# A decoder block's down product as seven block products by Strassen's algorithm

## The chip, the core and the metric

The kernel runs on one core of a Trainium2 chip. A core has TensorE for matrix products (PE in the profile, PEld for its weight loads), VectorE (DVE), ScalarE (ACT) and GpSimd (POOL) for work on elements, and SyncE (SP), which here issues nearly all transfers between the core's memory and DRAM, in the order of its own queue. Each engine works through its own instructions in a fixed order and waits for the others by semaphores. The metric is the time of one execution in microseconds (us).

## The reference

One decoder block over 1024 tokens of width 1024 in float32: eight heads of sparse attention, eight stick-breaking heads, an output projection, and a gated MLP with a convolution of width 3 along the tokens. The part that is changed is the last product:

```
gate, val = up[..., :D_FF], up[..., D_FF:]
h = h + (jax.nn.silu(gate) * val) @ w_down[layer]     # (1024 x 2816) @ (2816 x 1024)
```

and then a final RMSNorm.

## The kernel before, in words

Products run in a reduced float32 form (fp32r). To keep the accuracy, each operand is split into a high half (a copy in fp32r, on ScalarE, L193) and a low half (the operand less the high half, L194), and a product is three matmuls: high by high, high by low, low by high.

The stages that matter here, in order of time:

**The stick-breaking heads** (`sb_attend`, 65 to 345 us). Four pairs of heads go through 48 chunks, numbered here from 1. For each chunk `sb_front` makes logits on TensorE, two sigmoids on ScalarE, a scan on VectorE (L436) and two multiplications on GpSimd (L439: `A <- A,tt`); two chunks later `sb_turn` transposes the products on TensorE (L455), and `sb_back` multiplies them with the values. Beside this, in the gaps of TensorE, the next pair's projections run (L219 to L221): their weights come by SP (L204, `wr <- w_in_d`), and GpSimd makes the low halves (`wl`, L194). So GpSimd has 96 multiplications `A` and the halves `wl` in one fixed order.

**The up stage** (`up`, to 1246 us) makes `act = silu(gate) * val`, 22 blocks of 128 of the 2816 columns, and stores them to `act_d` in DRAM. Its product already runs as seven block products.

**The down stage** (`down`, from 1246.6 us). Two passes over the tokens (c, 512 tokens each); in a pass eight accumulators in PSUM (four blocks of 128 tokens `tb`, two halves `hf` of 512 output columns) take 22 blocks `i` of the contraction, each with three matmuls:

```
nc.tensor.matmul(pd, ah[:, s], dh[:, cs], start=i == 0, stop=False)
nc.tensor.matmul(pd, ah[:, s], dl[:, cs], start=False, stop=False)
nc.tensor.matmul(pd, al[:, s], dh[:, cs], start=False, stop=i == NF - 1)
```

That is 2 x 22 x 8 x 3 = 1056 matmuls of 128 x 512. `load_w` loads 128 rows of `w_down` (`wr`) and splits them (`dh` on ScalarE, `dl` on GpSimd); `load_act` loads 512 tokens of one act block (`ar`) and splits them (`ah` on ScalarE, `al` on VectorE). The first four blocks of a pass and the last four run accumulator by accumulator, so that the ends can be finished one by one: add to `h` (L1622), squares, a power on GpSimd, scale, store (L1572).

A scheduler sets each engine's order when the kernel is built, and moves instructions ahead of others where it reckons that they are ready; a tile with one buffer is written again only when its last reader is done.

Of the kernel before, what the change touches and what calls it, by code (L numbers as in the profile page):

```python
# [10 lines left out]
F32 = mybir.dt.float32  # L11
F32R = mybir.dt.float32r
# [68 lines left out]
class Kern:  # L81
# [479 lines left out]
                    nc.vector.memset(self.score[rows, i, cur + 1:16], NEG)  # L561


    def compress_in(self, kv, wp, vp):

        nc, a = self.nc, self.a
        w = self.load_cols(wp, a["w_in"], (C_KC, C_VC)[kv], bufs=3, rbufs=2, parts=2)
        for c in range(2):
            pm = self.ps("mm")
            yield from self.mm3_steps(pm, [w[k] + self.u(k, c) for k in range(KT)])  # L570
            src = self.tl(vp, [P, 512], "vt")
            nc.scalar.activation(src, pm, AF.Copy)
            nc.sync.dma_start(self.kct_d[kv][:, c * 512:c * 512 + 512], src)
            yield
# [491 lines left out]
    def run(self):  # L1066
# [15 lines left out]
        with self.pool("sbv", "right") as vp:  # L1082
            st_b, st_a = ExitStack(), ExitStack()
            stk = [None, st_b.enter_context(self.pool("stkb", "right"))]
            stk[0] = st_a.enter_context(self.pool("stka", "right"))
            ops = []
            with self.pool("xin") as xin:
                proj = self.sb_project(0, wp, stk[0], vp, ops, xin)
                self.load_norm(xin, vp, mxs, proj, stk[1])
                for _ in proj:  # L1090
                    pass
            with self.pool("sbw") as work:
                fill, due = iter(()), 0.0
# [19 lines left out]
                for _ in fill:  # L1113
                    pass
            st_a.close()
            st_b.close()
# [148 lines left out]
    def mlp(self, mxs):  # L1265
# [125 lines left out]
        for _ in fill:  # L1391
            pass
        st_r.close()
        self.weights, self.acts = {}, {}
        self.up(p1)
        self.down(st_up)

# [58 lines left out]
    def up(self, p1):  # L1456
# [3 lines left out]
        for i in range(NF):  # L1460
# [34 lines left out]
            if last:  # L1495
                for _ in range(AHEAD):
                    self.prepare()
                self.load_w(0)
                self.load_w(1)
            bb = self.ps(tags[1])  # L1500
            self.product(bb, i, "P6", True)
            u2 = self.scratch()
# [3 lines left out]
            u3 = self.scratch()  # L1506
            nc.vector.tensor_add(u3, bc, u2)
            if last:
                for j in range(GROUP):
                    if j > 1:  # L1510
                        self.load_w(j)
                    self.load_act(j, 0)
            bd = self.ps(tags[3])
            self.product(bd, i, "P5", True)

# [14 lines left out]
            gate(1)  # L1530


    def load_w(self, i):

        homes = ((self.qn, 0), (self.qn, 4), (self.mts, 4), (self.mts, 0))
        if i < 2 * len(homes):
            if i in self.weights:
                return
            t, lo = homes[i // 2]
            v = t[:, lo:lo + 4].rearrange("p a b t -> p (a b t)")[:, 2048 * (i % 2):2048 * (i % 2) + 2048]  # L1540
            dh, dl = v[:, 0:T], v[:, T:2048]
        else:
            dh, dl = (self.tl(self.dp, [P, T], t, 5, F32R) for t in ("dh", "dl"))
        raw = self.tl(self.rawp, [P, KT, P], "wr", 4).rearrange("p k c -> p (k c)")
        self.nc.sync.dma_start(raw, self.a["w_down"][i * P:(i + 1) * P, :])
        self.split_w(raw, dh, dl)
        self.weights[i] = (dh, dl)

    def load_act(self, i, c):

        if c == 0 and i < GROUP:
            raw = self.scratch()
            ah, al = (t[:, i, :] for t in self.R["P7"])
        else:
            raw = self.tl(self.dp, [P, 512], "ar", 3)
            ah, al = (self.tl(self.dp, [P, 512], t, 7, F32R) for t in ("ah", "al"))
        self.nc.sync.dma_start(raw, self.act_d[i][:, c * 512:c * 512 + 512])
        self.split_w(raw, ah, al, self.nc.vector)
        self.acts[i, c] = (ah, al)

    def down(self, st_up):
        nc, a = self.nc, self.a
        weights, acts = self.weights, self.acts
        rows = []

        def finish(tb, y, ss):
            r = self.rstd(ss, 1, 1.0 / DM, True)
            nc.scalar.activation(y[:, 0:512], y[:, 0:512], AF.Copy, scale=r[:, 0:1])
            nc.vector.scalar_tensor_tensor(y[:, 512:DM], hs[tb][:, 512:DM], r[:, 0:1], self.fnw[:, 512:DM],
                                           op0=ALU.mult, op1=ALU.mult)  # L1570
            for i in range(2):
                nc.sync.dma_start(a["out"][tb * P:(tb + 1) * P, i * 512:i * 512 + 512], y[:, i * 512:i * 512 + 512])  # L1572

        hs = {}
        with ExitStack() as st_2:
            for c in range(2):
                banks = {}

                def mms(i, tb, hf):
                    if (tb, hf) not in banks:  # L1580
                        banks[tb, hf] = self.ps(("o", "z", "z", "z", "mb", "tr", "tr", "ma")[2 * tb + hf])
                    pd = banks[tb, hf]
                    ah, al = acts[i, c]
                    dh, dl = weights[i]
                    s, cs = slice(tb * P, tb * P + P), slice(hf * 512, hf * 512 + 512)
                    nc.tensor.matmul(pd, ah[:, s], dh[:, cs], start=i == 0, stop=False)  # L1586
                    nc.tensor.matmul(pd, ah[:, s], dl[:, cs], start=False, stop=False)  # L1587
                    nc.tensor.matmul(pd, al[:, s], dh[:, cs], start=False, stop=i == NF - 1)  # L1588

                def blocks(first, last, alone):  # L1590

                    for i in range(first, last):
                        if (i, c) not in acts:
                            self.load_w(i)
                            self.load_act(i, c)
                        if not alone:
                            continue
                        for tb in range(4):
                            for hf in range(2):
                                mms(i, tb, hf)  # L1600

                blocks(0, GROUP, False)
                for tb in range(4):
                    for hf in range(2):
                        for i in range(GROUP):
                            mms(i, tb, hf)
                if c == 0:
                    st_up.close()
                    self.dp = self.rawp = st_2.enter_context(self.pool("dp"))
                    self.fnw = self.tl(self.dp, [P, DM], "fnw")  # L1610
                    nc.sync.dma_start(self.fnw, a["final_norm_w"].rearrange("(o c) -> o c", o=1).to_broadcast([P, DM]))
                blocks(GROUP, NF - GROUP, True)
                blocks(NF - GROUP, NF, False)
                for tb in range(4):
                    row = 4 * c + tb
                    h = hs[row] = self.tl(self.dp, [P, DM], "h", 4)
                    nc.sync.dma_start(h, self.h_d[row])
                    for hf in range(2):
                        for i in range(NF - GROUP, NF):
                            mms(i, tb, hf)  # L1620
                        cs = slice(hf * 512, hf * 512 + 512)
                        nc.vector.tensor_add(h[:, cs], banks[tb, hf], h[:, cs])  # L1622
                    y = self.tl(self.dp, [P, DM], "y", 3)
                    nc.gpsimd.tensor_mul(y[:, 0:512], h[:, 0:512], self.fnw[:, 0:512])
                    ss = self.square_sums(self.tl(self.nt, [P, 512], "na", 2), [h[:, 0:512], h[:, 512:DM]])
                    rows.append((row, y, ss))
                    if len(rows) > 1:
                        finish(*rows.pop(0))
            while rows:
                finish(*rows.pop(0))  # L1630


_INS = ["x", "norm1_w", "w_in", "cmp_pos_k", "cmp_pos_v", "cmp_k_w1", "cmp_k_w2", "cmp_v_w1", "cmp_v_w2",
# [27 lines left out]
```

## Time and profile before

| | |
|---|---|
| time, median of 3 runs | 1496.9 us (1496.57 to 1500.63) |
| the profiled execution: time, span | 1497.54 us, 1495.8 us |
| TensorE busy | 1436.6 us, 96% of the span |
| VectorE, ScalarE, GpSimd busy | 979.2, 793.6, 760.5 us |
| TensorE's granted clock, mean | 0.988 |

Matmuls are pipelined: a matmul's row lasts 0.39 us, but the next one starts 0.23 us after it. So a busy TensorE is read by the distance of its starts, and a wait by a start that comes later than that. The profiled execution is 0.6 us above the median of the runs.

### The profile page before, as it was taken

What the parts mean: (1) busy time and instruction counts of PE and PEld (TensorE: products, weight loads), DVE (VectorE), ACT (ScalarE), POOL (GpSimd) and SP (SyncE); (2) the same over time, 40 slices, a digit from 0 to 9 for tenths busy, and PEclk for the clock granted to TensorE, in tenths of its full rate; (3) what the DMA queues carried; (4) which work ended last, traced back from release to release, by engine and by line L of the source; (5) the groups of instructions that cost most, each with busy time, mean ns of one, the idle gap of its engine ahead of it and who ended that gap; (6) DMA issues with size and microseconds to landing.
All of it is one profiled execution on the core that took longest, in us unless ns stands there. A gap on an engine that the chain in (4) does not pass through costs nothing. (4 is left out here: it accounts for less than half of the span.)

```text
span 1495.8 us, 21914 instructions
## 1 busy us (share of the span) xinstructions
PE 1436.6 (96%) x7619; PEld 1203.4 (80%) x7619; DVE 979.2 (65%) x2018; ACT 793.6 (53%) x1691; POOL 760.5 (51%) x727
## 2 busy tenths in 40 slices
PE   7999999999899999999998999999999999999998
PEld 5777777777698888998887778888888887888886
DVE  5587878775247889998438687777877775414112
ACT  5576676653358888887323544444444453324122
POOL 3355655562326667664132466666666664545043
PEclk8999999999899999999999999999999999999999
DMA  5200100325311010003340222222222233845321
GB/s 194 70 22 22 29 22 22 96 64 162 112 29 30 2 57 2 1 15 113 127 131 25 71 85 85 85 85 85 85 80 83 85 113 113 290 146 186 109 93 57
DMA packets 113354, 122.75 MB, mean 82 GB/s; under 512 B 6988, under 2 KB 84444, under 8 KB 112988
## 3 DMA queue, kind: packets, MB, share of 16 engines
q1 hardware_dynamic: 113244, 121.36, 25.4%
q8 instruction: 60, 0.98, 0.3%
q14 instruction: 50, 0.41, 0.1%
HBM read 96.58 MB, written 24.75 MB: 81 GB/s over the span
## 5 line engine op out<-in xcount | busy, mean ns | idle before, releaser
L194 POOL TENSOR_TENSOR gl<-mxs,gh 128x512 fp32r<-128x512 f32 x88 | 116.6, 1326 | 67.9 <-ACT gh L193 64.7
L439 POOL TENSOR_TENSOR A<-A,tt 128x384 f32<-128x384 f32 (+3 forms) x96 | 95.8, 1003 | 97.1 <-DVE tt L436 50.5
L194 POOL TENSOR_TENSOR gl<-wr,gh 128x512 fp32r<-128x512 f32 x66 | 85.8, 1302 | 103.5 <-ACT gh L193 87.2
L194 DVE TENSOR_TENSOR al<-ar,ah 128x512 fp32r<-128x512 f32 x40 | 42.4, 1072 | 128.6 <-ACT ah L193 110.5
L194 POOL TENSOR_TENSOR dl<-wr,dh 128x1024 fp32r<-128x1024 f32 x28 | 69.4, 2485 | 103.1 <-ACT dh L193 90.9
L186 DVE TENSOR_TENSOR pl<-ps_tr,ph 128x512 fp32r<-128x512 f32 (+1 forms) x175 | 112.0, 643 | 13.2 <-ACT ph L185 11.8
L185 ACT ACTIVATE ph<-ps_tr 128x512 fp32r<-128x512 f32 (+1 forms) x175 | 98.0, 563 | 42.1 <-PE ps_tr L455 25.0
L193 ACT ACTIVATE gh<-mxs 128x512 fp32r<-128x512 f32 x88 | 55.3, 629 | 64.9 <-PE ps_ma L1453 22.0
L436 DVE TENSOR_TENSOR_SCAN tt<-tt 128x384 f32<-128x384 f32 (+1 forms) x64 | 69.8, 1093 | 28.4 <-ACT tt L429 27.8
L193 ACT ACTIVATE ah<-ar 128x512 fp32r<-128x512 f32 x40 | 25.0, 629 | 110.9 <-PE ps_ma L1587 98.7
L194 POOL TENSOR_TENSOR wl<-wr,wh 128x512 fp32r<-128x512 f32 x40 | 54.4, 1364 | 49.8 <-ACT wh L193 49.6
L429 ACT ACTIVATE tt<-ps_z 128x384 f32<-128x384 f32 (+3 forms) x96 | 47.6, 496 | 42.9 <-PE ps_z L428 20.2
L732 POOL TENSOR_SCALAR lgw<-lgw,r,gates 128x640 f32<-128x640 f32 (+4 forms) x64 | 48.3, 764 | 36.4 <-DVE r L730 14.7
L219 PE MATMUL ps_ma<-uh,wh 128*128 128x512 f32 x136 | 60.1, 442 | 5.6 <-ACT wh L193 5.6
L193 ACT ACTIVATE gh<-wr 128x512 fp32r<-128x512 f32 x66 | 40.9, 623 | 44.0 <-DMA wr<-w_up_d 15.5
L220 PE MATMUL ps_ma<-ul,wh 128*128 128x512 f32 x136 | 55.8, 410 | 3.0 <-DVE ul L189 3.0
L221 PE MATMUL ps_ma<-uh,wl 128*128 128x512 f32 x136 | 55.5, 408 | 0.1
L455 PE MATMUL ps_tr<-ident,A 128*128 128x128 f32 x320 | 49.1, 277 | 6.3 <-DVE pl L186 2.7
L455 PEld LDWEIGHTS ps_tr<-ident,A 128*128 128x128 f32 x320 | 37.1, 141 | 16.1 <-DVE osb L501 3.2
L1481 ACT ACTIVATE na<-na 128x512 f32<-128x512 f32 x44 | 27.6, 628 | 39.9 <-DVE na L1477 39.9
L1432 DVE TENSOR_TENSOR mxs<-mxs,wr 128x512 f32<-128x512 f32 x22 | 35.2, 1602 | 19.6 <-POOL mxs L1431 19.6
L430 ACT ACTIVATE A<-ps_z 128x384 f32<-128x384 f32 (+3 forms) x96 | 47.4, 493 | 0.1
(683 smaller groups left out, 5197.0 us busy)
## 6 DMA issues: line engine op xcount, KB each, us to landing
wr<-w_up_d SPq DMA_DIRECT2D x44, 512.0 KB, 5.0
wr<-w_down_d SPq DMA_DIRECT2D x36, 512.0 KB, 5.6
act_d<-na SPq DMA_DIRECT2D x44, 256.0 KB, 3.9
wr<-w_in_d SPq DMA_DIRECT2D x40, 256.0 KB, 4.2
ar<-act_d SPq DMA_DIRECT2D x40, 256.0 KB, 2.5
h<-h_d SPq DMA_DIRECT2D x8, 512.0 KB, 4.4
out_d<-y SPq DMA_DIRECT2D x16, 256.0 KB, 2.1
mxs<-x_d SPq DMA_DIRECT2D x4, 512.0 KB, 3.4
```

Source lines behind the costliest of these rows:

```text
L185: nc.scalar.activation(hi, src, AF.Copy)
L186: nc.vector.tensor_sub(lo, src, f(hi))
L193: nc.scalar.activation(hi, raw, AF.Copy)
L194: (eng or nc.gpsimd).tensor_sub(lo, raw, f(hi))
L219: nc.tensor.matmul(out, lh, rh, start=(i == 0), stop=False)
L220: nc.tensor.matmul(out, lh, rl, start=False, stop=False)
L221: nc.tensor.matmul(out, ll, rh, start=False, stop=(i == last))
L429: nc.scalar.activation(tt[:, 0:w], z[:, :w], AF.Sigmoid, scale=-1.0)
L436: nc.vector.tensor_tensor_scan(rev, rev, rev, 1.0 if carry[j] is None else carry[j], op0=ALU.mult, op1=ALU.bypass)
L439: nc.gpsimd.tensor_mul(A[:, j, 0:w], A[:, j, 0:w], tt[:, 1:w + 1])
L455: nc.tensor.transpose(pt[:, kk * 256 + j * P:kk * 256 + (j + 1) * P], A[:, j, c0:c0 + P], self.ident)
L732: nc.gpsimd.tensor_scalar(lg[i][:, :L], lg[i][:, :L], r[:, i:i + 1], gate[:, i:i + 1], op0=ALU.mult, op1=ALU.mult)
```

## The change

The down product's operands are cut in two along the tokens, along the contraction (11 blocks `j` each) and along the output columns, and the eight block products become seven (`DOWN`), each of sums of blocks. One block product has 11 steps of 4 token blocks x 3 matmuls = 12 matmuls.

- `fetch(n)` issues the loads of step n (77 steps); `halves(n)` makes the sums of act blocks on VectorE (L1609 to L1621) and splits both operands, the low halves now all on VectorE. Eight places in `qn` and `mts` take the halves of eight steps.
- `evacuate` takes a finished block product out of PSUM (28 times), `bring` adds parts on GpSimd (12 times), `finish` is as before.
- The four sums of w_down blocks come from DRAM tiles `td`. `down_sums` makes them during the stick-breaking heads: 22 rounds, each of two loads of 256 KB into one tile `ts` (one buffer), four additions on GpSimd (L577, L579, L581, L583), and one store of 512 KB. `sb_attend`'s loop calls it once at each of its steps.

```diff
+    def down_sums(self, pool):
+        nc = self.nc
+        src = self.a["w_down"].rearrange("(b i p) (h q c) -> b i q p h c", b=2, p=P, h=2, q=2)
+        self.td = [self.dram.tile([P, 4, 512], F32, name=f"td{j}") for j in range(NF // 2)]
+        for j in range(NF // 2):
+            for q in range(2):
+                t = self.tl(pool, [P, 4, 256], "ts")
+                for b in range(2):
+                    nc.sync.dma_start(t[:, 2 * b:2 * b + 2, :], src[b, j, q])
+                for _ in range(6):
+                    yield
+                b11, b12, b21, b22 = (t[:, i, :] for i in range(4))
+                nc.gpsimd.tensor_sub(b22, b12, b22)
+                yield
+                nc.gpsimd.tensor_sub(b12, b12, b11)
+                yield
+                nc.gpsimd.tensor_sub(b11, b11, b22)
+                yield
+                nc.gpsimd.tensor_sub(b21, b21, b11)
+                yield
+                yield
+                nc.sync.dma_start(self.td[j][:, :, 256 * q:256 * q + 256], t)
+                for _ in range(3):
+                    yield
...
+                sums = self.down_sums(work)
                 for _ in self.sb_attend(start, work, mxs):
+                    next(sums, None)
...
+    DOWN = ("P1", "P6", "P2", "P7", "P5", "P4", "P3")
+    def fetch(self, n):
...
+        if name == "P1":
+            v = act(0, 0, self.scratch() if n < GROUP else keep("a11"))
+        elif name == "P6":
+            v = act(0, 1, passing())
+            act(1, 1, keep("a22"))
+            if j < GROUP:
+                act(0, 0, keep("a11"))
+        elif name in ("P2", "P3"):
+            v = act(1, 0, passing())
+        w = self.scratch()
...
+    def halves(self, n):
...
+        if name == "P6":
+            s2 = kept["s2", j] = self.tl(self.dp, [P, 512], "s2", self.ND)
+            nc.vector.tensor_add(s2, v, kept["a22", j])
+            nc.vector.tensor_sub(s2, s2, kept["a11", j])
+            v = s2
+        elif name == "P7":
+            v = self.tl(self.dp, [P, 512], "ar", 4)
+            nc.vector.tensor_sub(v, kept["s2", j], kept["a22", j])
+        elif name == "P5":
+            v = self.tl(self.dp, [P, 512], "ar", 4)
+            nc.vector.tensor_add(v, kept["s2", j], kept["a11", j])
+        elif name == "P4":
+            v = kept["a22", j]
+        elif name == "P3":
+            nc.vector.tensor_sub(v, v, kept["s2", j])
...
+        self.split_w(v, ah, al, nc.vector)
+        self.split_w(w, bh, bl, nc.vector)
...
     def down(self, st_up):
...
+        def mms(n, tb):
...
+            nc.tensor.matmul(bank, ah[:, s], bh, start=first and j == 0, stop=False, skip_group_check=not first)
+            nc.tensor.matmul(bank, ah[:, s], bl, start=False, stop=False, skip_group_check=not first)
+            nc.tensor.matmul(bank, al[:, s], bh, start=False, stop=j == ND - 1, skip_group_check=not first)
```

GpSimd's order in the heads, around the 8th multiplication `A`. `ts` is the tile of a round's four additions, here those of rounds 3 and 4; `wl` is a low half for the projections. Before:

```order
L439 TENSOR_TENSOR A_672<-A_672,tt_699 128x512
L439 TENSOR_TENSOR A_712<-A_712,tt_713 128x256
L439 TENSOR_TENSOR A_712<-A_712,tt_738 128x256
L439 TENSOR_TENSOR A_768<-A_768,tt_769 128x384
L439 TENSOR_TENSOR A_768<-A_768,tt_806 128x512
L194 TENSOR_TENSOR wl_925<-wr_923,wh_924 128x512
```

And now:

```order
L439 TENSOR_TENSOR A_727<-A_727,tt_728 128x256
L577 TENSOR_TENSOR ts_965<-ts_965 128x256
L579 TENSOR_TENSOR ts_965<-ts_965 128x256
L581 TENSOR_TENSOR ts_965<-ts_965 128x256
L583 TENSOR_TENSOR ts_965<-ts_965 128x256
L439 TENSOR_TENSOR A_727<-A_727,tt_756 128x256
L439 TENSOR_TENSOR A_787<-A_787,tt_788 128x384
L439 TENSOR_TENSOR A_787<-A_787,tt_828 128x512
L577 TENSOR_TENSOR ts_1118<-ts_1118 128x256
L194 TENSOR_TENSOR wl_952<-wr_950,wh_951 128x512
L579 TENSOR_TENSOR ts_1118<-ts_1118 128x256
```

Nothing of the old work changed its order; the additions were put in between. Seven multiplications stand ahead of round 3 and 64 of the 96 ahead of round 22, the last: 57 multiplications stand among 19 rounds, three in each on the average.

The DMA queue of SP in the heads; `wr` are the projections' weights, `ts` a round's two loads, `td` its store. Before, only the weights stood here:

```order
L204 DMA wr_917<-w_in_d 128x4x128
L204 DMA wr_923<-w_in_d 128x4x128
L204 DMA wr_1186<-w_in_d 128x4x128
L204 DMA wr_1192<-w_in_d 128x4x128
L204 DMA wr_1373<-w_in_d 128x4x128
```

And now:

```order
L587 DMA td_618<-ts_816 512x1x256
L573 DMA ts_965<-w_down_d 128x2x256 x2
L587 DMA td_619<-ts_965 512x1x256
L573 DMA ts_1118<-w_down_d 128x2x256 x2
L204 DMA wr_1234<-w_in_d 128x4x128
L587 DMA td_619<-ts_1118 512x1x256
L573 DMA ts_1278<-w_down_d 128x2x256 x2
L204 DMA wr_1422<-w_in_d 128x4x128
```

A round's store waits for its additions, the next round's loads wait for that store, and the weights stand in line between them.

VectorE's order in the down stage. Before, one low half per act block (`al`); now, in the second block product, two sums (L1609, L1610) and two low halves (L194) for each step:

```order
L194 TENSOR_TENSOR al_13983<-ar_13981,ah_13982 128x512
L194 TENSOR_TENSOR al_14019<-ar_14017,ah_14018 128x512
L194 TENSOR_TENSOR al_14055<-ar_14053,ah_14054 128x512
L194 TENSOR_TENSOR al_14091<-ar_14089,ah_14090 128x512
L194 TENSOR_TENSOR al_14127<-ar_14125,ah_14126 128x512
```

```order
L1609 TENSOR_TENSOR s_14018<-ar_13965,a_13967 128x512
L194 TENSOR_TENSOR qn<-mxs,qn 128x512
L1610 TENSOR_TENSOR s_14018<-s_14018,a_13758 128x512
L1609 TENSOR_TENSOR s_14042<-ar_13989,a_13991 128x512
L1610 TENSOR_TENSOR s_14042<-s_14042,a_13761 128x512
L194 TENSOR_TENSOR qn<-s_14018,qn 128x512
L194 TENSOR_TENSOR qn<-mxs,qn 128x512
```

The sums of the next step stand between the halves of this one, so that VectorE does not wait for ScalarE's high half of a sum that it has just made.

## Rows read from the trace of the kernel before

**Rows 1.** The profile's page: span, busy us by engine, PE in 40 slices

```profile
span 1495.8 us, 21914 instructions
...
PE 1436.6 (96%) x7619; PEld 1203.4 (80%) x7619; DVE 979.2 (65%) x2018; ACT 793.6 (53%) x1691; POOL 760.5 (51%) x727
...
PE   7999999999899999999998999999999999999998
```

**Rows 2.** TensorE in order of time: the down stage's start, its one gap, its end

```profile
1246.62 0.39 PE L1586 MATMUL ps_o<-qn,P7h 128*128 128x512 f32 x1
...
1268.60 0.39 PE L1587 MATMUL ps_o<-mts,ah 128*128 128x512 f32 x1
1271.19 0.50 PE L1588 MATMUL ps_o<-mts,al 128*128 128x512 f32 x1 [2.20 <-DVE al L194]
...
1488.26 0.39 PE L1588 MATMUL ps_ma<-dh,al 128*128 128x512 f32 x1
```

**Rows 3.** Busy us of each engine (and instructions) in three stretches

```profile
core 0: us, PE busy (x) PEld busy (x) DVE busy (x) ACT busy (x) POOL busy (x), PEclk, DMA share, GB/s
77.40:245.70 168.30, 163.40 (x960) 133.05 (x959) 131.56 (x230) 116.65 (x247) 95.16 (x110) 1.00 0.10 24
1246.60:1488.60 242.00, 239.80 (x1057) 197.93 (x1055) 69.05 (x83) 74.72 (x115) 95.09 (x54) 1.00 0.44 150
1488.60:1495.80 7.20, 0.05 (x1) 0.00 (x0) 1.60 (x3) 1.44 (x3) 0.82 (x3) 0.69 0.23 86
```

**Rows 4.** GpSimd: multiplications 6 to 8, 65 and 66 of the heads

```profile
75.42 2.90 POOL L439 TENSOR_TENSOR A<-A,tt 128x512 f32<-128x512 f32 x3
...
245.67 0.87 POOL L439 TENSOR_TENSOR A<-A,tt 128x384 f32<-128x384 f32 x1 [0.96 <-DVE tt L432]
...
248.26 1.09 POOL L439 TENSOR_TENSOR A<-A,tt 128x512 f32<-128x512 f32 x1 [1.72 <-ACT tt L429]
```

**Rows 5.** TensorE: the transposes that take chunk 33's products

```profile
253.70 0.61 PE L455 MATMUL ps_tr<-ident,A 128*128 128x128 f32 x4
```

**Rows 6.** The DMA queue of SP at the start of the down stage

```profile
1229.38 26.01 SPq L1483 DMA_DIRECT2D act_d<-na  x4
1255.97 0.39 SPq L1545 DMA_DIRECT2D wr<-w_down_d  x1
1256.45 0.38 SPq L1557 DMA_DIRECT2D ar<-act_d  x1
```

**Rows 7.** DMA issues in four stretches: count, KB each, us to landing

```profile
w<-cmp_k_w_d SPq DMA_DIRECT2D x5, 256.0 KB, 2.6
...
bcmp_d<-KB SPq DMA_DIRECT2D x1, 480.0 KB, 2.6
...
mx_d<-mxs SPq DMA_DIRECT2D x4, 512.0 KB, 4.5
...
wq<-w_in_d SPq DMA_DIRECT2D x4, 512.0 KB, 3.5
```

**Rows 8.** A split's subtraction alone, one beside GpSimd, and the split's groups

```profile
1451.05 0.69 DVE L194 TENSOR_TENSOR al<-ar,ah 128x512 fp32r<-128x512 f32 x1 [4.75 <-ACT ah L193]
...
1277.29 2.17 DVE L194 TENSOR_TENSOR al<-ar,ah 128x512 fp32r<-128x512 f32 x1 [2.08 <-ACT ah L193]
...
1276.50 2.40 POOL L194 TENSOR_TENSOR dl<-wr,dh 128x1024 fp32r<-128x1024 f32 x1 [3.11 <-ACT dh L193]
...
L193 ACT ACTIVATE ah<-ar 128x512 fp32r<-128x512 f32 x40 | 25.0, 629 | 110.9 <-PE ps_ma L1587 98.7 <-DMA ar<-act_d 12.1
```

**Rows 9.** GpSimd's groups from 77.4 to 245.7 us: count, busy us, mean ns

```profile
L194 POOL TENSOR_TENSOR wl<-wr,wh 128x512 fp32r<-128x512 f32 x16 | 22.6, 1411 | 5.6 <-ACT wh L193 5.5
L439 POOL TENSOR_TENSOR A<-A,tt 128x256 f32<-128x256 f32 x15 | 11.0, 736 | 9.1 <-DVE tt L436 4.7 <-DVE tt L432 3.1 <-ACT ph L185 1.2
```

**Rows 10.** The last hand-over from VectorE to GpSimd

```profile
1490.23 0.16 DVE L1226 TENSOR_TENSOR ss<-ss 128x1 f32<-128x1 f32 x1 [0.85 <-ACT na L1224]
1490.48 0.19 POOL L169 TENSOR_SCALAR rv<-ss 128x1 f32<-128x1 f32 x1 [1.80 <-DVE ss L1226]
```

More of the change, by code (lines that the diff above doesn't have):

```diff
@@ L1113, in run @@
                 for _ in fill:
+                    pass
+                for _ in sums:
                     pass
@@ L1393, in mlp @@
         st_r.close()
-        self.weights, self.acts = {}, {}
+        self.raw_ab, self.kept, self.slots = {}, {}, {}
         self.up(p1)
@@ L1497, in up @@
                     self.prepare()
-                self.load_w(0)
-                self.load_w(1)
+                for n in range(2):
+                    self.fetch(n)
+                    self.halves(n)
             bb = self.ps(tags[1])
@@ L1508, in up @@
             if last:
[L1509 to L1512, printed above, removed]
+                for n in range(2, GROUP):
+                    self.fetch(n)
+                    self.halves(n)
             bd = self.ps(tags[3])
@@ L1530, in up @@
             gate(1)
[L1533 to L1559, printed above, removed]
-    def down(self, st_up):
[L1562 to L1574, printed above, removed]
-        with ExitStack() as st_2:
[L1576 to L1602, printed above, removed]
-                for tb in range(4):
[L1604 to L1630, printed above, removed]
@@ new lines, in halves @@
+    def halves(self, n):
+        nc = self.nc
+        name, j = self.DOWN[n // self.ND], n % self.ND
+        v, w = self.raw_ab.pop(n)
+        kept = self.kept
+        if name == "P6":
[13 more added lines that the diff above has]
+            nc.vector.tensor_sub(v, v, kept["s2", j])
+        t, lo = ((self.qn, 0), (self.qn, 4), (self.mts, 4), (self.mts, 0))[n % 8 // 2]
+        place = t[:, lo:lo + 4].rearrange("p a b t -> p (a b t)")[:, n % 2 * 2048:n % 2 * 2048 + 2048]
+        ah, al, bh, bl = (place[:, 512 * i:512 * i + 512] for i in range(4))
+        self.split_w(v, ah, al, nc.vector)
+        self.split_w(w, bh, bl, nc.vector)
+        self.slots[n] = (ah, al, bh, bl)
@@ new lines, in down, with more, residual, evacuate @@
+    def down(self, st_up):
+        nc, a, ND = self.nc, self.a, self.ND
+        tags = (("o", "z", "z", "z"), ("mb", "tr", "tr", "ma"))
+        fetched = made = GROUP
+        banks, p1, u3, out = [None, None], [], [], {}
+        pending = []
+        def more(n):
+            nonlocal fetched, made
+            while fetched < min(n + 7, 7 * ND):
+                self.fetch(fetched)
+                fetched += 1
+            while made < min(n + 5, 7 * ND):
+                self.halves(made)
+                made += 1
+        def mms(n, tb):
+            first = self.DOWN[n // ND] in ("P1", "P6", "P7", "P5")
+            bank = banks[n // ND % 2][tb]
+            ah, al, bh, bl = self.slots[n]
+            s = slice(tb * P, tb * P + P)
+            j = n % ND
+            nc.tensor.matmul(bank, ah[:, s], bh, start=first and j == 0, stop=False, skip_group_check=not first)
+            nc.tensor.matmul(bank, ah[:, s], bl, start=False, stop=False, skip_group_check=not first)
+            nc.tensor.matmul(bank, al[:, s], bh, start=False, stop=j == ND - 1, skip_group_check=not first)
+        def residual(key, tag, c, tb, hf):
+            t = out[4 * c + tb, hf] = self.tl(self.dp, [P, 512], tag, 4 if tag == "h0" else ND)
+            nc.sync.dma_start(t, self.h_d[4 * c + tb][:, 512 * hf:512 * hf + 512])
+            return t
+        def evacuate(name, tb):
+            bank = banks[self.DOWN.index(name) % 2][tb]
+            if name == "P1":
+                p1.append(self.tl(self.dp, [P, 512], "p1", 4))
+                nc.scalar.activation(p1[tb], bank, AF.Copy)
+            elif name == "P6":
+                nc.vector.tensor_add(p1[tb], bank, p1[tb])
+            elif name == "P2":
+                h = residual(name, "h0", 0, tb, 0)
+                nc.vector.tensor_add(h, bank, h)
+            elif name == "P7":
+                u3.append(self.tl(self.dp, [P, 512], "u3", 4))
+                nc.vector.tensor_add(u3[tb], bank, p1[tb])
+            else:
+                h = out[{"P5": (4 + tb, 1), "P4": (4 + tb, 0), "P3": (tb, 1)}[name]]
+                nc.vector.tensor_add(h, bank, h)
+        def bring(name):
+            for tb in range(4):
+                if name == "P5":
+                    h, u = residual(name, "a11", 1, tb, 1), u3[tb]
+                elif name == "P4":
+                    h, u = residual(name, "a11", 1, tb, 0), p1[tb]
+                else:
+                    h, u = residual(name, "a22", 0, tb, 1), p1[tb]
+                nc.gpsimd.tensor_add(h, h, u)
+        def finish(row):
+            if row is not None:
+                h = [out[row, i] for i in range(2)]
+                y = self.tl(self.dp, [P, DM], "y", 2)
+                nc.gpsimd.tensor_mul(y[:, 0:512], h[0], self.fnw[:, 0:512])
+                ss = self.square_sums(self.tl(self.nt, [P, 512], "na", 2), h)
+                pending.append((row, h, y, ss))
+            if pending and (row is None or len(pending) > 1):
+                row, h, y, ss = pending.pop(0)
+                r = self.rstd(ss, 1, 1.0 / DM, True)
+                nc.scalar.activation(y[:, 0:512], y[:, 0:512], AF.Copy, scale=r[:, 0:1])
+                nc.vector.scalar_tensor_tensor(y[:, 512:DM], h[1], r[:, 0:1], self.fnw[:, 512:DM],
+                                               op0=ALU.mult, op1=ALU.mult)
+                for i in range(2):
+                    nc.sync.dma_start(a["out"][row * P:(row + 1) * P, i * 512:i * 512 + 512], y[:, i * 512:i * 512 + 512])
+        with ExitStack() as st_2:
+            for i, name in enumerate(self.DOWN):
+                if name in ("P1", "P6", "P7", "P5"):
+                    banks[i % 2] = [self.ps(t) for t in tags[i % 2]]
+                n0 = i * ND
+                j0 = 0
+                if i == 0:
+                    for tb in range(4):
+                        for n in range(GROUP):
+                            mms(n, tb)
+                    st_up.close()
+                    self.dp = st_2.enter_context(self.pool("dp"))
+                    j0 = GROUP
+                for j in range(j0, ND - GROUP if name == "P3" else ND):
+                    more(n0 + j)
+                    if i == 0 and j == j0:
+                        self.fnw = self.tl(self.dp, [P, DM], "fnw")
+                        nc.sync.dma_start(self.fnw, a["final_norm_w"].rearrange("(o c) -> o c", o=1).to_broadcast([P, DM]))
+                    if j == 6 and name in ("P4", "P3"):
+                        bring(name)
+                    if name == "P3" and 2 <= j < 6:
+                        finish(4 + j - 2)
+                    for tb in range(4):
+                        mms(n0 + j, tb)
+                if name == "P3":
+                    more(n0 + ND - 1)
+                    for tb in range(4):
+                        for j in range(ND - GROUP, ND):
+                            mms(n0 + j, tb)
+                        evacuate(name, tb)
+                        finish(tb)
+                    finish(None)
+                    break
+                if name == "P5":
+                    bring(name)
+                for tb in range(4):
+                    evacuate(name, tb)
```

17 lines of the change are left out of this document (added).

## The prediction

> **What bounds the kernel now.** I read the page first: TensorE is busy in 96% of the span, and its row of slices has a 9 nearly everywhere [rows 1]. Since matmul rows overlap, that alone does not say that TensorE sets the pace, so I went to the down stage, in order of time. The first matmul starts at 1246.62 us, the last of 1056 at 1488.26: 1055 distances in 241.64 us. One of them is long, 1268.60 to 1271.19, where VectorE's `al` was late [rows 2]; against the usual distance of 0.23 us it costs 2.36. The rest gives 239.28 / 1055 = 0.2268 us per matmul, without another wait. So this stage is TensorE's own: each matmul less is worth 0.227 us as long as the operands come. After the last one, 7.2 us of finishing follow [rows 3].
>
> Then the heads, where the change puts the new sums. From 77.4 to 245.7 us TensorE is busy for 163.4 of 168.3 us, GpSimd for 95.2 and VectorE for 131.6 [rows 3]. GpSimd looks half free. But its multiplications stand in the chain of each chunk: the second of chunk 33 (multiplications 65 and 66) ends at 249.35 [rows 4], and TensorE transposes the products from 253.70 on [rows 5], 4.35 us later. This is the slack; what GpSimd is late beyond it, TensorE waits. It has 4.9 us of gaps in this window, so lost time does not come back.
>
> **The change part by part.** *Matmuls.* 7 x 11 x 12 = 924 instead of 1056: 132 x 0.2268 = 29.9 us less.
>
> *The gap at 1271.* In SP's queue the act loads of the first pass stood behind the last stores of the up stage: SP was held there from 1229.38 until 1255.4, and the first `ar` went out at 1256.45 [rows 6]. In the new order the first three of these loads stand ahead of the last two stores. The first four steps now last 48 x 0.227 = 10.9 us instead of 21.8, so step 5 is wanted at about 1257.5. From about 1250 on its load (2.6 us, as for the 256 KB in [rows 7]) and its split (0.63 and 0.69 us [rows 8]) fit. I take the gap as gone: 2.4 us less; if step 5 is late instead, the loss is as large again.
>
> *Splits and sums of the down stage.* VectorE gets 154 low halves and 55 sums of 128 x 512, and 24 evacuations of about the same price. A subtraction takes 0.69 us alone and 2.17 us beside GpSimd's 2.40 us subtraction of the same kind [rows 8]. GpSimd's `dl` go away, and in place of them it has 12 additions and the 8 rows' finishing, so I take 0.69: 233 x 0.69 = 161 us under 924 x 0.2268 = 209.6. ScalarE: 154 x 0.63 [rows 8] = 97 us. Both have cover on the whole. The tightest stretch is the second block product: four operations a step, 2.76 us, for 12 x 0.2268 = 2.72 us of TensorE. Over 11 steps that is half a microsecond, and eight places for halves hold more than that. I cost this at nothing; without the cover see the rivals. Transfers: 77 weights and 59 act blocks of 256 KB and the rows of `h` and the output, some 43 MB in 210 us or 205 GB/s, against 150 GB/s now [rows 3]; not a bound. The end keeps its 7.2 us: per row the same evacuation, squares, power and scale, and rows now come each 2.7 us with about 2.2 us of ScalarE work.
>
> *The sums in the heads.* This decides. A round cannot overlap with the next: one tile, so additions, store, loads, additions follow each other, through three hand-overs. GpSimd's order fixes how many multiplications come between, and whatever stands behind the next round's first addition waits with it for the loads. Between round 3 and round 22 stand 57 multiplications; before, they ran from the end of the 8th, 75.42 + 2.90 = 78.32, to the end of the 65th, 245.67 + 0.87 = 246.54 [rows 4]. So a round has 168.2 / 19 = 8.85 us if nothing is to be delayed. A round needs:
>
> - four additions of 128 x 256; the nearest row is the multiplication of that size, 736 ns [rows 9]: 2.94 us.
> - what the new order puts between its first and last addition: in 19 groups five `wl` (1.41 us each [rows 9]), six multiplications and seven short ones, by estimate 14.6 us together: 0.77 us a round.
> - a store of 512 KB. Below, 480 KB stored alone: 2.6 us; above, four stores of 512 KB issued in a row: 4.5 [rows 7]. It runs alone, but in pieces of 1 KB, so I take 3.1.
> - two loads of 256 KB. One alone in the same shape takes 2.6; two go out about 0.5 us apart [rows 6] and share the engines, so at least 3.1; one load of 512 KB takes 3.5 [rows 7]. I take 3.2; with the weights' loads between them, up to 4.0.
> - three hand-overs; the last one from VectorE to GpSimd takes 1490.48 - 1490.39 = 0.09 us [rows 10]: 0.3.
>
> Sum 10.3 us; with the bounds of the transfers 9.7 to 12.5. The stage gets longer by 19 x (10.3 - 8.85) = 27.6 us, less the slack that the additions themselves leave, 4.35 - 2.94 = 1.4, once: 26.2 us. During the 6.3 us of transfers GpSimd has (95.2 - 14.6) / 19 = 4.2 us of other work, so it waits for the transfers, not they for it.
>
> The Trainium skill, GPSIMD Engine Reference, "3.1 Elementwise — side-by-side cycle accounting", gives a two-input elementwise operation 2.6 cycles an element at 1.2 GHz; an estimate from it is 0.56 us for 256 elements, 2.2 us for the four, a round of 9.6 us and a loss of 13 us. The row of 736 ns is longer than that, and I go by the row. The Trainium skill, DMA: Bandwidth & Descriptors, "Anatomy of one DMA — SWDGE (gpsimd) path", fits 2.0 us plus the bytes at 436 GB/s, for another path than SP's; by it the store would be 3.2 us, and the loss 28 us.
>
> *Sum.* 1497.5 (the profiled execution's own time) - 29.9 - 2.4 + 26.2 = 1491.4; the median stands 0.6 lower: 1490.8, so 1491 us.
>
> **The rivals.** *The sums are hidden.* If a round needs no more than the 8.85 us, the whole 32.3 us stay: 1465 us. For it: GpSimd is idle for 43% of the window. Against: even with the shortest transfers the terms give 9.7, and one would have to be half as long as its row. Up to 9.1 us it is 1465 to 1468.
>
> *The rounds cost more than the product gives back (slower).* Place: SP's queue, where the projections' weights `wr` stand between a store and the next loads and wait for their own buffer, which GpSimd frees. Each such wait, and a store as slow as 4.5 us, lengthens the round. From (32.3 + 1.4) / 19 + 8.85 = 10.6 us on nothing is gained; with the slow store (11.7 us) the heads lose 53 us: 1518. For it: the scheduler put the additions as early as it reckoned possible, so every error about the transfers is paid in each round. Against: the store is alone in its queue.
>
> *VectorE bounds the down stage.* If each sum were followed by a wait for ScalarE's copy of it (0.63 us and a hand-over of 0.09 twice), a step of the second product would take 3.6 us instead of 2.72, and 11 steps 9.5 us more: 1500 us with the heads as forecast. The order printed above speaks against it.
>
> **How the numbers follow.** A round between 9.5 and 10.9 us, forecast: 0.55, from 1475 to 1501 by the same sum, which is the likeliest case's own range. Hidden sums: 0.12. Longer rounds: 0.25. VectorE in the down stage: 0.08. The likeliest is 1491. The range from 1466 to 1515 leaves out the fully hidden case's edge and the slowest stores, less than 2 in 10. About 0.3%, 4.5 us, is what a measurement of this kernel can tell from no change. Faster than 1492.4: 0.32 of the forecast's 0.55, the hidden sums, and 0.02 of VectorE's case, 0.46. Within: 0.20 + 0.03 = 0.23. Slower than 1501.4: 0.25 + 0.03 + 0.03 = 0.31.
>
> **What would show it.** Matmuls of the down stage: 924, still 0.227 us apart, from first to last about 210 us. No gap over 1 us near its twelfth microsecond. The additions L577 at about 0.74 us, and their starts from round 3 to round 22 some 195 us apart instead of 168; the idle time before them put down to the loads of `ts`. The heads' end near 371 us instead of 345, and all later stages moved by that amount. I am wrong if the rounds follow at 9 us or less, if TensorE waits in the down stage for low halves, or if the delay of the heads comes from VectorE's scans instead of the loads.

## The result, and the profile after

The change made the kernel slower: 1532.0 us, median of four runs (1529.6 to 1533.1), against 1497.0; the ratio is 1.023, with a 95% interval of 1.0215 to 1.0244. The profiled execution took 1533.13 us. Its page, with the lines that answer to [rows 1], and the issues of the new transfers (count, KB each, median us to landing):

```profile
span 1531.1 us, 22357 instructions
...
PE 1429.6 (93%) x7487; PEld 1194.4 (78%) x7487; DVE 1076.8 (70%) x2191; ACT 820.6 (54%) x1769; POOL 761.7 (50%) x791
...
PE   7988778799979999999999989999999999999997
...
ts<-w_down_d SPq DMA_DIRECT2D x44, 256.0 KB, 2.9
td<-ts SPq DMA_DIRECT2D x22, 512.0 KB, 3.1
```

TensorE has lost its nines in the third to the eighth slice, 77 to 306 us: those lie in the heads. The down stage answers to [rows 2]; TensorE there, first and last matmul:

```profile
1312.81 0.39 PE L1655 MATMUL ps_o<-qn 128*128 128x512 f32 x1
...
1522.02 0.39 PE L1657 MATMUL ps_z<-mts 128*128 128x512 f32 x1
```

924 matmuls in 209.21 us, 0.2267 us from one to the next over the whole stage, so the old gap is gone and no new one came: 32.4 us less than the 241.64 of before. From the first matmul to the end of the span it is 218.29 us against 249.18: 30.9 us gained. But the stage begins at 1312.81 instead of 1246.62, 66.2 us late. The transposes of the heads (L455) show where: the last one starts at 408.6 us instead of 341.6, 67.0 us late. Nothing after the heads adds to it: 66.2 - 30.9 = 35.3, the difference of the spans.

One round of the sums in the changed kernel, on GpSimd and in SP's queue (start, duration, the idle time before it and what ended it):

```profile
92.75 0.74 POOL L577 TENSOR_TENSOR ts<-ts 128x256 f32<-128x256 f32 x1 [2.91 <-DMA ts<-w_down_d]
93.44 1.29 POOL L194 TENSOR_TENSOR wl<-wr,wh 128x512 fp32r<-128x512 f32 x1
94.68 0.75 POOL L579 TENSOR_TENSOR ts<-ts 128x256 f32<-128x256 f32 x1
95.51 0.73 POOL L581 TENSOR_TENSOR ts<-ts 128x256 f32<-128x256 f32 x1
96.18 0.21 POOL L441 MEMSET A<- 128x128 f32 x1
96.34 0.73 POOL L583 TENSOR_TENSOR ts<-ts 128x256 f32<-128x256 f32 x1
97.03 1.09 POOL L439 TENSOR_TENSOR A<-A,tt 128x512 f32<-128x512 f32 x1
...
104.38 0.76 POOL L577 TENSOR_TENSOR ts<-ts 128x256 f32<-128x256 f32 x1 [1.68 <-DMA ts<-w_down_d]
```

```profile
97.11 0.57 SPq L587 DMA_DIRECT2D td<-ts  x1
100.20 1.20 SPq L573 DMA_DIRECT2D ts<-w_down_d  x2
```

The additions end at 97.07, the store goes out at 97.11, the loads 3.09 us later, when it has landed, and the next addition starts 4.18 us after that: a round of 11.63 us. Over the 19 rounds from the third to the last the starts of L577 run from 81.07 to 310.71, 12.09 us each where 8.85 were to be had. What GpSimd waited for between these two (us, times, longest), and the groups of the additions:

```profile
POOL ts L577 <- DMA ts<-w_down_d: 53.3, 16, 6.1
```

```profile
L581 POOL TENSOR_TENSOR ts<-ts 128x256 f32<-128x256 f32 x19 | 18.0, 948 | 1.3
L577 POOL TENSOR_TENSOR ts<-ts 128x256 f32<-128x256 f32 x19 | 16.1, 846 | 58.4 <-DMA ts<-w_down_d 53.3 <-PE ps_tr L455 5.1
L579 POOL TENSOR_TENSOR ts<-ts 128x256 f32<-128x256 f32 x19 | 15.9, 836 | 0.9
L583 POOL TENSOR_TENSOR ts<-ts 128x256 f32<-128x256 f32 x19 | 14.6, 766 | 1.2
```

GpSimd, which works through its order, stood still for the loads in 16 of 19 rounds, with the multiplications of the heads behind it.

### The profile page after: what moved, and what is told of

It reads as the page before. It is cut to its first block, busy times and chain, and to the rows that moved or that the text cites. A ratio compares the mean times of both kernels' runs of the same rounds, so it can differ in the third digit from the quotient of the medians.

```text
span 1531.1 us, 22357 instructions
## 1 busy us (share of the span) xinstructions
PE 1429.6 (93%) x7487; PEld 1194.4 (78%) x7487; DVE 1076.8 (70%) x2191; ACT 820.6 (54%) x1769; POOL 761.7 (50%) x791
## 5 line engine op out<-in xcount | busy, mean ns | idle before, releaser
L194 POOL TENSOR_TENSOR gl<-mxs,gh 128x512 fp32r<-128x512 f32 x88 | 116.4, 1324 | 70.3 <-ACT gh L193 67.0
L194 POOL TENSOR_TENSOR gl<-wr,gh 128x512 fp32r<-128x512 f32 x66 | 85.8, 1301 | 103.4 <-ACT gh L193 84.9
L186 DVE TENSOR_TENSOR pl<-ps_tr,ph 128x512 fp32r<-128x512 f32 (+1 forms) x175 | 111.7, 641 | 13.2 <-ACT ph L185 11.9
L455 PE MATMUL ps_tr<-ident,A 128*128 128x128 f32 x320 | 55.1, 298 | 48.3 <-DVE pl L186 22.3
L455 PEld LDWEIGHTS ps_tr<-ident,A 128*128 128x128 f32 x320 | 39.8, 151 | 61.9 <-DVE pl L186 19.5
L1690 POOL TENSOR_TENSOR a<-a,p 128x512 f32<-128x512 f32 x8 | 12.3, 1538 | 139.5 <-DVE mts L194 120.9
L194 POOL TENSOR_TENSOR wl<-wr,wh 128x512 fp32r<-128x512 f32 x40 | 54.1, 1358 | 34.7 <-ACT wh L193 34.5
L219 PE MATMUL ps_ma<-uh,wh 128*128 128x512 f32 x136 | 63.2, 465 | 5.6 <-ACT wh L193 5.6
L577 POOL TENSOR_TENSOR ts<-ts 128x256 f32<-128x256 f32 x22 | 18.7, 852 | 70.0 <-DMA ts<-w_down_d 64.9
L219 PE MATMUL ps_mb<-late,wh 128*128 128x512 f32 x112 | 49.3, 440 | 0.0
L436 DVE TENSOR_TENSOR_SCAN tt<-tt,tt 128x256 f32<-128x256 f32 (+1 forms) x32 | 39.1, 1221 | 14.4 <-ACT tt L429 8.4
L1464 DVE TENSOR_TENSOR mxs<-mxs,wr 128x512 f32<-128x512 f32 x22 | 35.3, 1602 | 19.7 <-POOL mxs L1463 19.6
```

Source lines behind the costliest of these rows:

```text
L186: nc.vector.tensor_sub(lo, src, f(hi))
L194: (eng or nc.gpsimd).tensor_sub(lo, raw, f(hi))
L219: nc.tensor.matmul(out, lh, rh, start=(i == 0), stop=False)
L436: nc.vector.tensor_tensor_scan(rev, rev, rev, 1.0 if carry[j] is None else carry[j], op0=ALU.mult, op1=ALU.bypass)
L455: nc.tensor.transpose(pt[:, kk * 256 + j * P:kk * 256 + (j + 1) * P], A[:, j, c0:c0 + P], self.ident)
```

## The experiments

Two theories of the lost 66 us: **W**, GpSimd waits for loads with the multiplications behind it; its rivals, that the additions' own work costs it (**G**, in the later runs split in **P**, GpSimd's work becomes the pace, and **C**, each addition delays TensorE by its own time), or the transfers and SP's queue (**Q**). Some kernels hold additions in place: `issue_after` fixes their place in GpSimd's order behind a given multiplication, without a wait for it. The order of all other instructions of the heads on TensorE, VectorE, ScalarE and GpSimd is the same in all kernels that have the sums there. Ratios are to the kernel before, run beside them; its medians in these comparisons lie between 1496.3 and 1499.4 us, so a difference between kernels of two comparisons is good to some 3 us.

**no_sums.** The gain alone.

```diff
-                sums = self.down_sums(work)
+                sums = iter(())
...
-                              "P6": self.td[j][:, 0, :], "P5": self.td[j][:, 1, :], "P4": self.td[j][:, 2, :],
+                              "P6": rows(0)[:, 512:DM], "P5": rows(1)[:, 512:DM], "P4": rows(0)[:, 0:512],
...
```

> Leaves out the sums in the heads; the down stage reads blocks of w_down where it read the sums, in transfers of the same size, so its output is not the reference's. It measures the gain of the down stage alone. The down stage, from its first matmul to the end of the span, took 249.2 us before and 218.3 after, 30.9 less; if all of the loss is in the heads, the time is 1497.0 - 30.9 = 1466 us (1463 to 1469), whichever theory holds. If a part of the loss lies elsewhere (the attention or up stages), it comes out above 1472.

1465.8 us, ratio 0.980 (0.9776 to 0.9823). The product is worth 30.6 us against the 1496.3 of before in that comparison, and all of the loss lies with the sums.

**adds_alone.** The work without the waits.

```diff
+                if j + q == 0:
+                    t = self.tl(pool, [P, 4, 256], "ts")
+                    for b in range(2):
+                        nc.sync.dma_start(t[:, 2 * b:2 * b + 2, :], src[b, j, q])
+                place = self.PLACES[2 * j + q]
+                while len(self.muls) < place:
+                    yield
...
+            with self.tc.issue_after(self.muls[place - 1]):
+                op(*args)
...
-                nc.sync.dma_start(self.td[j][:, :, 256 * q:256 * q + 256], t)
```

> Leaves out all transfers of the sums but the first two loads: the 88 additions stand at the same places among GpSimd's multiplications, on one tile, and wait for nothing; the down stage reads blocks of w_down (output not the reference's). Theory W (GpSimd waits in its fixed order for the loads of ts): the work of the additions alone fits, 1466 to 1480 us. Rival G (the additions' own work, and their contention with VectorE, delays the multiplications): most of the loss of 66 us stays, 1510 us or more.

1486.9 us, ratio 0.993 (0.9918 to 0.995): between the two. The additions cost 21.1 us with nothing to wait for. Its rounds 3 to 22 (columns as in [rows 3]), and the group of the additions there:

```profile
76.89:262.60 185.71, 164.99 (x947) 132.85 (x946) 135.47 (x226) 113.77 (x241) 163.97 (x184) 0.98 0.09 22
```

```profile
L571 POOL TENSOR_TENSOR ts<-ts 128x256 f32<-128x256 f32 x76 | 70.8, 932 | 4.2
```

GpSimd is busy for 163.97 of 185.71 us. A round is 185.71 / 19 = 9.77 us long, and an addition takes 0.93 us on the average, not 0.74.

**same_places_two_tiles.** The waits taken away, the order kept.

```diff
-                t = self.tl(pool, [P, 4, 256], "ts")
+                t = self.tl(pool, [P, 4, 256], "ts", 2)
...
+    PLACES = (0, 0, 7, 10, 13, 16, 19, 22, 24, 26, 29, 32, 35, 38, 42, 45, 48, 51, 53, 57, 60, 64)
```

> The whole computation, with two tiles ts instead of one, and each round's additions held at the same place among GpSimd's multiplications as in the changed kernel, so that only the loads come earlier. A tile then has two rounds' program, 17.7 us, for its cycle of 12.1. Theory W: additions find their data there, 1466 to 1482 us. Rival G: no change, about 1532. Rival Q (the transfers in SP's queue delay the projections' weights): 1500 us or more.

1487.5 us, ratio 0.994 (0.9922 to 0.9952): 44.6 us below the changed kernel, and within 0.6 of adds_alone, whose order on GpSimd is the same, so the transfers cost nothing more. It missed W's range by 5.5 us, which is the additions' work: adds_alone took as long. After the first round GpSimd does not wait for `ts` once (idle us and times, from the view of the tile):

```profile
  DMA ts<-w_down_d: 7.0, 1
```

**four_apart.** The same rounds, farther apart.

```diff
+    PLACES = (0, 4, 8, 12, 16, 20, 24, 28, 32, 36, 40, 44, 48, 52, 56, 60, 64, 68, 72, 76, 80, 84)
```

> The whole computation, one tile as in the changed kernel, but each round's additions held behind four more multiplications instead of three. Four multiplications were 4 x 168.2 / 57 = 11.8 us of the heads before; a round took (310.71 - 81.07) / 19 = 12.1. Theory W: about 21 x 0.3 = 6 us are lost and a few at single rounds: 1470 to 1485 us. Rival G and rival Q: the same additions and transfers, nearly the same loss, over 1515.

1496.8 us, ratio 1.000 (0.9983 to 1.001). 35 us less than the changed kernel by the places alone, which G and Q did not expect; but 12 us above W's range. I had left out the additions' work, and the waits cost more than the 6 us I had reckoned: four_apart_two_tiles, below, puts them at 17.0. GpSimd still sat idle for loads 13 times:

```profile
  DMA ts<-w_down_d: 28.9, 13
```

**transfers_alone.** The four additions left out, all transfers kept.

```diff
-                nc.gpsimd.tensor_sub(b22, b12, b22)
-                yield
...
+                for _ in range(4):
+                    yield
```

> Leaves out the 88 additions and keeps every transfer: what is stored is what was loaded (output not the reference's). The loads of a round still wait for the store before, on one tile, and the projections' weights stand among them in SP's queue. Theories W and P: no engine waits for these transfers, so the heads go at their old pace, 1465 to 1470 us. Rival Q (SP's queue and the transfers themselves delay the weights): 1475 us or more.

1464.7 us, ratio 0.978 (0.976 to 0.9801): Q is out. The whole chain of stores and loads is free as long as no engine with other work behind it waits for it.

**half_the_additions.** As adds_alone, with two additions a round; the edit is against adds_alone.

```diff
-                self.behind(place, nc.gpsimd.tensor_sub, b11, b11, b22)
                 yield
-                self.behind(place, nc.gpsimd.tensor_sub, b21, b21, b11)
                 yield
```

> Leaves out the same transfers as adds_alone and two of each round's four additions (output not the reference's); nothing waits for a transfer. The 88 additions alone cost 21 us. Theory P (GpSimd's work becomes the pace: 5.0 us of old work a round, four additions of 0.93 us and 1.1 us of idling in turns make 9.8 us where 8.85 were to be had): two additions make 5.0 + 1.9 + 1.1 = 8.0, under 8.85, so nearly nothing is lost, 1466 to 1471 us. Theory C (each addition delays the multiplication behind it, and TensorE, by its own time): half the loss, 1474 to 1479 us.

1468.5 us, ratio 0.980 (0.9771 to 0.9836): 2.8 us above no_sums (6.8 between the spans of the two profiled executions, of which this run's was the slowest of four) where four additions cost 21. Halving the work took away far more than half of the loss; C, which had 1474 or more, is out.

**two_tiles_free_order.** The one-word cure, without holding the order.

```diff
-                t = self.tl(pool, [P, 4, 256], "ts")
+                t = self.tl(pool, [P, 4, 256], "ts", 2)
```

> The whole computation with two tiles ts and nothing else changed, so that the scheduler may move the rounds: it puts all 22 rounds ahead of the 32nd multiplication (1.4 multiplications a round, where the changed kernel had three). Theory W alone (waits): two rounds share a cycle of 12.1 us, about 6.1 a round, and the multiplications among them had 4.1 us a round: 22 x 2 = 44 us lost, 1510 us. Theory P: GpSimd's work of a round, 3.7 us of additions and 1.4/3 of 5.0, is 6.1 as well: the same 1510. If the two tiles by themselves were the cure, 1466 to 1487.

1518.5 us, ratio 1.013 (1.0096 to 1.0167). The scheduler used the second tile to pull the rounds together, and most of the loss stayed; the last L577 starts at 201.3 us instead of 310.7. It is 8.5 us above the 1510 that both W and P had reckoned, so it does not tell them apart. GpSimd waited 28.8 us for loads and was busy for 118.7 of the 147.8 us of the rounds (56.7 to 204.5), so waits and work both fill them.

**four_apart_two_tiles.** Both edits.

> The whole computation, additions held four multiplications apart and two tiles. No additions wait for loads, so the 28.9 us that GpSimd sat idle for them in four_apart are free. Theory P: a round of 11.8 us holds 6.7 us of old work, 3.7 of additions and 1.5 of idling in turns, 11.9: about 2 to 8 us lost, 1468 to 1474 us. Theory C: the 88 additions cost the same 21 us wherever they stand, 1487 us.

1479.8 us, ratio 0.987 (0.9835 to 0.9908). 17.0 us below four_apart, the waits; 14.0 above no_sums (10.9 when each is taken against the before of its own comparison), more than P's 2 to 8 and less than C's 21. The additions cost more the closer they stand, but P's sizes are not confirmed: with GpSimd busy for 149.42 of 173.00 us, delays still reach TensorE.

```profile
77.00:250.00 173.00, 160.57 (x932) 130.19 (x931) 131.53 (x225) 112.16 (x237) 149.42 (x168) 0.99 0.35 110
```

**sums_in_up.** Another place.

```diff
+        sums = self.down_sums(self.gran)
         for i in range(NF):
...
+            next(sums, None)
             bb = self.ps(tags[1])
...
+                self.tc.keep_in_program_order(nc.gpsimd.tensor_sub(*args))
+                yield
```

> The whole computation; the 22 rounds are taken out of the heads and put into the up stage, one in each of its 22 blocks of some 19.6 us, on one tile, held in their places in GpSimd's order. There GpSimd is busy for 223 of 430 us and a round of 12.1 us is shorter than a block; the halves that it makes there are up to six ahead of TensorE. If only the place in the heads was wrong, 1466 to 1472 us. Rival: VectorE, busy for 345 of the 430 us there, is slowed by the additions beside it (0.69 us alone, 2.17 beside GpSimd) and TensorE waits: 1475 us or more.

1470.4 us, ratio 0.981 (0.9781 to 0.9842), inside the first range: the best whole kernel of the study, 29.0 us below the before run beside it. The additions run at 0.74 us (median), GpSimd waits for a load once, for 1.0 us, and from 900 to 1200 TensorE does 443 matmuls in each 100 us, as in no_sums.

**sums_in_up_late.** The rounds begin at the fourth block, seven steps a block instead of six.

```diff
+            step = lambda: next(sums, None) if i >= 3 else None
...
-            next(sums, None)
+            step()
```

> The whole computation; as sums_in_up, which was 4.7 us above no_sums and lost them between 850 and 900 us, in the first blocks of the up stage. Here the rounds begin at the fourth block and take the other 19, so a round has 16.8 us instead of 19.6, still more than 12.1. If those 4.7 us were lost to the first rounds standing ahead of the first halves, 1465 to 1468 us; if they are the price of the additions wherever they stand in this stage, 1470 us again.

1496.2 us, ratio 0.999 (0.9974 to 1.0006): a miss, in which the first mechanism came back. In both kernels a round has six steps, and two of them lie between its store and loads and the next round's first addition. In sums_in_up these were always the same two of a block's six, 8.85 us in nearly every round. With seven steps a block they fall at another place in each block; store and loads take about 7.3 us, and most places have less:

```profile
POOL ts L579 <- DMA ts<-w_down_d: 37.9, 17, 4.5
```

**late_but_loaded.** As sums_in_up_late, with four steps from the loads to the first addition, and for that the additions in pairs; the edit is against sums_in_up_late.

```diff
-            yield
+            for _ in range(3):
+                yield
...
-                yield
+                if k % 2:
+                    yield
```

> The whole computation; sums_in_up_late, which took 1496.2 us and in which GpSimd sat idle for loads of ts 17 times, 37.9 us in all, with one thing changed: the first addition of a round stands four steps behind the loads (some 11 us) instead of two, and two additions stand together. The rounds begin and end at the same blocks. Theory W: the additions find their data, 1466 to 1470 us. If the later and denser rounds themselves cost the 26 us (more work for GpSimd and VectorE in each block), it stays at 1490 or more.

1477.9 us, ratio 0.987 (0.9839 to 0.9897). The waits fell from 37.9 to 3.5 us and 18.3 us came back, which is W in another stage. The time lies between the two ranges; 7.5 us above sums_in_up are left, and whether they are the price of the denser rounds or of the pairs was not tested.

## Why the prediction was wrong

**What held.** *Matmuls* and *the gap*: 32.3 us forecast, 32.4 measured from first to last matmul. Splits and sums of the down stage: TensorE never waited for them. The mechanism in the heads, one tile, a store and loads between two groups of additions, GpSimd held in its order, is what the rows show, and taking away only the wait gave back 44.6 us. The waits of TensorE's transposes in the heads end mostly at VectorE (L186, 22.3 us, and L432, 14.0; at the multiplications A, 9.7), neither of them a scan, which the prediction had named as a sign against it; that GpSimd stands behind them is shown by same_places_two_tiles, not by these rows. The store was 3.1 us, as taken. That the additions alone take the 0.74 us of [rows 9] is luck: 736 ns there is a mean that some long ones raise; over the whole of the heads before, the 24 multiplications of that size have a median of 0.64 us, and the additions are slower than that.

**The step that failed** is "Sum 10.3 us", the length of a round. It was 12.09, and the terms that were mis-sized are the loads, 4.58 us from the first load's issue to the next round's first addition for the 3.2 taken, and the additions, 3.40 for 2.94; what stands between them was 0.78, as taken (0.77), and from the last addition to the first load it was 3.33. The loads alone make 1.4 of the 1.8 us.

I had put the two loads between the 2.6 us of one and the 3.5 of a load of 512 KB. In fact the second goes out 0.6 us after the first, and it takes longer. Few landings are recorded: in the changed kernel those of four first loads, 2.9 to 3.0 us after their issue, and of one second load, 4.0 us, with the addition 0.12 us behind the landing. In four_apart all five that are recorded are second loads, 3.3 to 4.0 us. So a pair that nothing disturbs takes 4.0 us or a little more (median 4.2). The mean is above that because in some rounds it was not yet GpSimd's turn, and because a load of the projections' weights held back the first load in one of the 19 rounds and the second in four, by 6.6 us in all.

With 12.09 the prediction's own formula gives 19 x 3.24 - 1.4 = 60.2 us; the first two rounds, which stand ahead of the first multiplication (72.2 us instead of 67.5), make 4.7 more: 64.9 of the 66.2 us. That this comes so near does not show that the loss has the formula's two parts alone, since without any wait the additions still cost 21 us.

The bounds in the text reached to 12.5, which by that formula is 1533 us, but the range stopped at 1515: every one of the 19 rounds pays for an error, and I gave the upper end of the bounds too little. The rival "the rounds cost more than the product gives back", at 0.25, is what came: the round was above its break-even of 10.6. Of the two reasons that it named, the store was not slow, and the weights made up 6.6 of the 34 us by which the 19 rounds were longer than forecast.

**What the argument lacked.** It counted only the chain, and reckoned the additions' own time as covered but for a slack of 1.4 us. Without any wait they cost 21 us: GpSimd is then busy for 88% of its rounds, a round takes 9.77 us where 8.85 were to be had, and an addition takes 0.93 us instead of 0.74. By the measured kernels, the product gains 30.6 us, the additions lose 21.1, the transfers 0.6 and the waits 44.6. These add up to the loss (35.7; 35.0 beside its own before) by construction, since each is the difference of two neighbouring kernels.

**A small miss.** The end was forecast at its old length; it is 9.08 us from the last matmul's start instead of 7.54. VectorE, in order of time:

```profile
1523.44 0.75 DVE L1703 SCALAR_TENSOR_TENSOR y<-a,ry,fnw 128x512 f32<-128x512 f32 x1 [0.95 <-POOL ry L170]
1524.11 0.68 DVE L1679 TENSOR_TENSOR a<-ps_z,a 128x512 f32<-128x512 f32 x1
```

The last evacuation stands behind the row before's last scaling and starts 2.09 us after the last matmul did, against 0.43 before (1488.69 after 1488.26).

## What to carry to other kernels

Side work on an engine that is half idle can cost the wait for its inputs in that engine's fixed order on top of its own time: compare the full cycle of its buffer, from addition over store and loads to addition, with the time that the work around it leaves, and pay the difference once per round. A second buffer helped here only with the order held (1487.5 us against 1518.5), since the scheduler, which reckoned the data ready, pulled the rounds together. And side work belongs where the engine runs ahead of the one that sets the pace (1470 us in the up stage), not where TensorE waits for it in turns; there too its loads need their time (1496.2 us in sums_in_up_late).

## What the runs showed of the hardware

GpSimd's addition of 128 x 256 takes 0.74 us alone, but 1.7 us where it starts together with a scan of VectorE. The changed kernel, GpSimd, then VectorE:

```profile
189.42 1.71 POOL L579 TENSOR_TENSOR ts<-ts 128x256 f32<-128x256 f32 x1
191.22 1.75 POOL L581 TENSOR_TENSOR ts<-ts 128x256 f32<-128x256 f32 x1
193.05 0.74 POOL L583 TENSOR_TENSOR ts<-ts 128x256 f32<-128x256 f32 x1
```

```profile
189.40 1.21 DVE L436 TENSOR_TENSOR_SCAN tt<-tt 128x512 f32<-128x512 f32 x1
...
191.17 1.28 DVE L436 TENSOR_TENSOR_SCAN tt<-tt,tt 128x512 f32<-128x512 f32 x1
```

Both long additions start with a scan and end half a microsecond after it; the third, without one, is short. The Trainium skill, SBUF — State Buffer, "SBUF: two separate sides", says that such a VectorE instruction with two inputs in SBUF and a GpSimd instruction that reads SBUF exclude each other for a whole instruction, whichever starts first; these rows agree in that the addition ends only behind the scan, though its end follows after 0.52 us and not after the 0.74 of a whole addition. How much of the 21 us is this, no run separates.

TensorE's granted clock fell where it was starved. In the changed kernel, two stretches of 10 us:

```profile
110.00:120.00 10.00, 9.10 (x54) 7.27 (x53) 5.62 (x9) 5.92 (x12) 3.73 (x5) 1.00 0.32 107
120.00:130.00 10.00, 6.46 (x24) 5.21 (x24) 2.80 (x5) 3.76 (x8) 6.42 (x9) 0.66 0.40 131
```

In the second the mean is 0.66. TensorE had started nothing from 118.71 to 122.58 us, and from 122 to 128 the granted clock is 0.50, the lower of its levels of 1.2 and 2.4 GHz; in the kernel before TensorE was busy for all of 120 to 130, at 1.00. From 67 us to the end of the heads (411 and 366 us) TensorE is busy for 289.2 us in the changed kernel (1560 matmuls, mean clock 0.93) and for 269.9 in same_places_two_tiles (1562, 0.99). So about 19 of the 44.6 us that the waits cost show as longer matmuls, and the rest as idle time. How many of the 19 would have been idle time at the higher clock, no run shows.
